# A decoder layer on one core: interleaving hi and lo of the stationary operands and reading the moving ones backwards in both FFNs

## The chip, the cores and the metric

The kernel runs on one core of a Trainium2 chip. TensorE multiplies: a matmul holds one operand still in its array (the stationary one, read from SBUF by a weight load of 128 columns, shown in the trace as PEld LDWEIGHTS) and streams the other (the moving one) past it, one column after the other; the sums go to PSUM. VectorE (DVE), ScalarE (ACT) and GpSimd (POOL) work element by element, SyncE (SP) starts most transfers. SBUF has 128 partitions; what is said below of places and steps is within a partition, in elements of four bytes.

The metric is the device time of one execution in microseconds. A profile is one execution with records of every instruction.

## The reference

One layer with 16 meta tokens and 256 sequence tokens, 272 positions of 2048 features, all in float32:

```python
h = h + 0.5 * swiglu(rms_norm(h, ffn1_norm_g), ffn1_w_gate, ffn1_w_up, ffn1_w_down)
u = rms_norm(h, mix_norm_g); z = u @ w_in          # q, k, v, q_idx, k_idx, w_idx, x_c, B, C, two gates
# sparse attention: the 64 best keys per query by an indexer, softmax over them
# short gated convolution; both branches gated, summed, projected
h = h + merged @ w_out
h = h + 0.5 * swiglu(rms_norm(h, ffn2_norm_g), ffn2_w_gate, ffn2_w_up, ffn2_w_down)
return h[:, N_META:]
```

with `swiglu(x, g, u, d) = (silu(x @ g) * (x @ u)) @ d` and 5632 hidden features. Each weight matrix is used once.

## The kernel before

Every matmul operand of the large products is split into a high part (the value rounded to the type float32r, which TensorE streams at full rate) and a low part (what is left). A product is then three matmuls, hi*hi, hi*lo and lo*hi, added up in the same PSUM bank.

*The stream of weights.* The class `Stream` (L68 on) carries all weights in the order of use. `load` brings chunks of 128 x 2048 elements from HBM into three raw buffers (L100, issued by SP). `split` (L106) takes blocks of 1024 columns: ACT writes the high part into a tile `whi` (L115), DVE the low part into a tile `wlo` (L116), four buffers of each. `next` hands out blocks in order, splits three blocks ahead (`AHEAD`), and runs the small work of other engines that was queued with `later` for that block. So TensorE's order is the program's order, and ACT and DVE work ahead of it by blocks.

*FFN 1* (`ffn_features`, L430) keeps features on partitions. The weights are stationary, 128 x 128 at a time, the activations are moving, 272 tokens at a time: `fmajor` (L292) calls `mac` (L286), whose three matmuls are L288 (whi with the high activations), L289 (whi with the low ones) and L290 (wlo with the high ones). The activations lie in `act` (L226), for each of 16 feature tiles a high and a low row of `PITCH` = 320 elements; the 272 tokens fill places 48 to 319, so that they end on a multiple of `LINE` = 64. The hidden features go to `mid` (L435) in rows of the same kind, in two halves (c = 0, 1) of 22 tiles; gate, up and down products are `pg`, `pu`, `pd`. The first two gate and up tiles run interleaved as `start_tiles`. `norm` (L391) adds the squares over partitions with two small matmuls against ones (L403); their result scales the columns of the gate and up products.

*The middle* (projections, attention, convolution, branches, output projection) uses the same stream, `fmajor`, `paired` and `tokens`. Its last step, `to_act` (L1056), writes the normed input of FFN 2, high and low part, back into the rows of `act`.

*FFN 2* (`ffn_tokens`, L487) has the roles exchanged: activations are stationary, 128 features x 128 tokens, and the weights move, 512 columns at a time. `tokens` (L308) issues for each of the two token tiles j and each block the three matmuls L316 (xhi, whi), L317 (xhi, wlo), L318 (xlo, whi). The stationary operands come from `act` through `act_tokens` (L321) for gate and up, and from `mid` (L490) for down; `mid` holds per feature tile 256 high elements and then 256 low ones, written by `split_into` (L339) at L535.

In both FFNs, high and low parts of a stationary operand lie in separate runs, each read with step one, and a stationary tile begins at a multiple of 64 elements of its SBUF tile. Every moving operand is read in ascending order.

Of the kernel before, what the change touches and what calls it, by code (L numbers as in the profile page):

```python
# [10 lines left out]
F32R = mybir.dt.float32r  # L11
# [51 lines left out]
LATER = LINE - META  # L63
SUB = 1024
RAW = 2048


class Stream:  # L68
# [14 lines left out]

    def add(self, src, n, width, cuts=()):

        per = min(SUB // width, SUB // P)
        g = len(self.loads)
        self.loads.append((src, n * width, cuts))
        at = [0, *cuts, n] if cuts else [*range(0, n, per), n]
        for a, b in zip(at, at[1:]):  # L90
            self.subs.append((g, a * width, b - a, width))

# [13 lines left out]
    def split(self, upto):  # L106
        nc = self.nc
        while self.n_split < min(upto, len(self.subs)):
            g, c, kk, width = self.subs[self.n_split]
            self.load(g + RAW_BUFS)  # L110
            n = kk * width
            raw = self.raw[g][:, c : c + n]
            hi = self.split_pool.tile([P, SUB], F32R, name="whi")
            lo = self.split_pool.tile([P, SUB], F32R, name="wlo")
            nc.scalar.activation(hi[:, :n], raw, AF.Copy)  # L115
            nc.vector.tensor_sub(lo[:, :n], raw, hi[:, :n].bitcast(F32))  # L116
            self.ready[self.n_split] = [
                (hi[:, i * width : (i + 1) * width], lo[:, i * width : (i + 1) * width]) for i in range(kk)
            ]
            self.n_split += 1  # L120
            if self.n_split == len(self.subs) or self.subs[self.n_split][0] > g:
                self.load(g + 1 + RAW_BUFS)
# [39 lines left out]
def tile_decoder_layer(  # L162
# [31 lines left out]

    def chunks(src, i0, i1, width=P):
        for i in range(i0, i1):
            st.add(src[i], RAW // width, width)

    st.add(wgu1[0], RAW // P, P, (4, 8, 12))
    st.add(wgu1[1], RAW // P, P, (4, 8))  # L200
    for c in range(2):
        chunks(wgu1, max(2, c * 2 * FHALF), (c + 1) * 2 * FHALF)
        chunks(wd1, c * FHALF, (c + 1) * FHALF)
    chunks(wk, 0, G)
# [102 lines left out]

    def tokens(ps_of, x, n):  # L308

        k = 0  # L310
        while k < n:
            blocks = [st.next()] + st.rest()
            for j, ps in ps_of.items():
                for i, (whi, wlo) in enumerate(blocks):
                    xhi, xlo = x(k + i, j, 0), x(k + i, j, 1)
                    nc.tensor.matmul(ps, xhi, whi, start=k + i == 0, stop=False)  # L316
                    nc.tensor.matmul(ps, xhi, wlo, start=False, stop=False)  # L317
                    nc.tensor.matmul(ps, xlo, whi, start=False, stop=k + i == n - 1)  # L318
            k += len(blocks)
# [70 lines left out]

    def norm(row, lag, cols=False):  # L391

        box = {}

        def two(x):
            return x.rearrange("p (a t) -> p a t", a=2)

        def total():
            nc.vector.tensor_add(ssq[0], ssq[0], ssq[1])

        def across():
            for i in range(2):
                nc.tensor.matmul(row[:, i], ones, two(ssq[0])[:, i], start=True, stop=True)  # L403
            box[0] = rsqrt(two(R), row, (P, T), 1.0 / D, two)

        def inverse():
            box[0][1]()
            if cols:
                nc.vector.tensor_mul(R2, R, R)
                turned(rcol[:, 0], R[:, :32], 0, 0)  # L410
                for q in range(4):
                    turned(
                        rcol[:, 1:3], R[:, META:].rearrange("p (j r b) -> p r j b", r=4, b=32)[:, q], q, q
                    )

        st.later(total, lag)
        st.early(across, lag + 1)
        st.later(lambda: box[0][0](), lag + 1)
        st.later(inverse, lag + 2)
# [10 lines left out]
    def ffn_features():  # L430

        n = T
        xhi, xlo = parts(LATER)
        with tc.tile_pool(name="ffn1", bufs=2, reuse_waits="tile") as fp:
            mid = fp.tile([P, FHALF, 2, PITCH], F32R, name="mid", bufs=1)  # L435
            i_hi, i_lo = (mid[:, :, i, PITCH - n :] for i in range(2))

# [13 lines left out]
            two = [aux_tile(f"start{i}") for i in range(2)]  # L451
            norm(two[0][:, :, T : T + T // 2], 13)
            least = st.at + 14
            for c in range(2):
                for f in range(FHALF):
# [13 lines left out]
                    st.later(lambda pu=pu, box=box: times(pu, box), 1 + side, least + 1)  # L469
                    st.later(lambda f=f, box=box: split_into(i_hi[:, f, :], i_lo[:, f, :], box["v"]), 2 + side, least + 1)  # L470
                for d in range(KD):
                    pd = mm_tile("pd")
                    fmajor(pd[:, :n], lambda k: i_hi[:, k, :], lambda k: i_lo[:, k, :], FHALF)
                    st.later(lambda d=d, pd=pd: add_to(h[:, d], pd, 0.5, False))
                    if c == 1:
                        st.later(lambda d=d: (next_act(d, gains[1], 0, LATER), square(d, 0)), 2)

    def turn_columns(mt, s, r):
# [8 lines left out]
    def ffn_tokens():  # L487

        with tc.tile_pool(name="ffn2", bufs=1, reuse_waits="tile") as fp:
            mid = fp.tile([P, 4 * GROUPS[0], 2, SEQ], F32R, name="mid")  # L490

# [30 lines left out]
            for c, n in enumerate(GROUPS):  # L522
                for f in range(n):
                    s = fp.tile([P, 2, 512], F32, name="s", bufs=2)
                    mt = fp.tile([P, 4, SEQ], F32, name="mt", bufs=2)
                    pg = {j: mm_tile(f"pg{j}") for j in (1, 2)}
                    tokens(pg, act_tokens, KD)
                    st.later(lambda pg=pg, s=s: gate(pg, s))
                    pu = {j: mm_tile(f"pu{j}") for j in (1, 2)}
                    tokens(pu, act_tokens, KD)  # L530
                    st.later(lambda pu=pu, s=s: times(pu, s))
                    for r in range(4):
                        st.later(lambda mt=mt, s=s, r=r: turn_columns(mt, s, r), 2 + r)
                    to = mid[:, 4 * f : 4 * f + 4]
                    st.later(lambda to=to, mt=mt: split_into(to[:, :, 0], to[:, :, 1], mt), 6)  # L535
                for d in range(D // 512):
                    pd = {j: mm_tile(f"pd{j}") for j in (1, 2)}
                    tokens(pd, lambda k, j, part: mid[:, k, part, (j - 1) * P : j * P], 4 * n)
                    for j in (1, 2):
# [24 lines left out]
    with ExitStack() as mix:  # L564
# [491 lines left out]
        def to_act(g, mt):  # L1056
            for f in range(4):
                d = 4 * g + f
                hi, lo = (act[:, d, i, LATER + META :][:, :SEQ] for i in range(2))
                gain = gains[2][:, d : d + 1]  # L1060
# [48 lines left out]


def _down_columns(w):
    cut = GROUPS[0] * 512
    return np.concatenate([_chunks(_tiles(w[:cut], 512)), _chunks(_tiles(w[cut:], 512))])

# [30 lines left out]
def _layout(x, meta_tokens, ffn1_norm_g, ffn1_w_gate, ffn1_w_up, ffn1_w_down, mix_norm_g, w_in, q_norm_g,  # L1145
# [31 lines left out]
    a["wo"] = _chunks(_tiles(w_out[0], 512))  # L1177
    gu = np.stack([_tiles(ffn2_w_gate[0], 512), _tiles(ffn2_w_up[0], 512)], 1)
    a["wgu2"] = _chunks(gu.reshape(-1, P, KD * 512))
# [21 lines left out]
```

## Time and profile before

| | |
|---|---|
| median of two runs | 2143.46 us (2143.18 to 2143.74) |
| span of the profiled execution | 2141.4 us |
| DMA | 397.58 MB, mean 186 GB/s |
| matmuls and weight loads recorded | 12902 each |
| FFN 1 | about 5 to 788 us of the span |
| middle | 788 to 1419 us |
| FFN 2 | 1419 us to the end |

The page of the profile begins with the busy time of each engine and its share of the span. Busy time of TensorE is no measure of its speed, because a matmul's record lasts longer than the distance to the next one: consecutive matmuls overlap. What matters on a TensorE that never waits is that distance, called a slot here. The page's groups (line, engine, operation, result<-operands, shapes, count | busy time, mean time of one in ns | idle time of the engine before them and what ended it) show counts and means; the view of stretches gives busy time and counts between two moments.

### The profile page before, as it was taken

To read this page: it belongs to the slowest core of one execution; us is meant where nothing else is said; L and a number is where in the kernel's file an instruction comes from. 1 tells how busy PE (TensorE), PEld (TensorE's weight loads), DVE (VectorE), ACT (ScalarE), POOL (GpSimd) and SP (SyncE) were. 2 spreads that over 40 slices of the span, in tenths; PEclk is the share of its full clock that TensorE was granted. 3 is DMA by queue.
4 is the path that set the end of the run, shared out by engine and by line. 5 is a ranking of instruction groups with operands and counts; after the bars stand their busy time and mean duration, and the time that the engine had idled before them with its cause. 6 is when DMAs were issued, how large, how long until landed. Compare 5 with 4: busy or idle time off the path is not lost.

```text
span 2141.4 us, 30929 instructions
## 1 busy us (share of the span) xinstructions
PE 2136.3 (100%) x12902; PEld 1921.2 (90%) x12902; DVE 1325.8 (62%) x1776; ACT 954.5 (45%) x1173; POOL 10.0 (0%) x28
## 2 busy tenths in 40 slices
PE   9999999999999999999999999999999999999999
PEld 9999999999999998799988888888888888888887
DVE  7555544455555556677686487886676644666664
ACT  6444433344444445565444444454444433444442
POOL 0000000000000000000000000000000000000000
PEclk9999999999999999999999999999999999999999
DMA  7555545555544545454555555555555555555554
GB/s 267 189 181 179 179 180 178 178 177 177 177 178 178 177 170 177 159 176 158 172 188 194 194 189 204 177 183 210 196 196 186 196 191 195 196 197 195 189 200 143
DMA packets 56909, 397.58 MB, mean 186 GB/s; under 512 B 6337, under 2 KB 7105, under 8 KB 9409
## 3 DMA queue, kind: packets, MB, share of 16 engines
q1 hardware_dynamic: 55872, 393.51, 53.4%
q8 instruction: 101, 1.65, 0.3%
q10 hardware_dynamic: 576, 1.05, 0.1%
q0 software_dynamic: 320, 1.05, 0.1%
q14 instruction: 40, 0.32, 0.0%
HBM read 393.49 MB, written 2.10 MB: 185 GB/s over the span
## 4 chain that ended last, share of the span: by engine, by line
PE 99%; DMA 0%; DVE 0%; SPq 0%; ACT 0%; issue 0%; ACTq 0%
PE pd L290 4%; PE pd L289 4%; PE pd L288 4%; PE pu L289 4%; PE pg L289 4%; PE pg L288 4%; PE pu L288 4%; PE pu L290 4%; PE pg L290 4%; PE pg L317 4%; PE pg L318 4%; PE pd L318 4%; PE pu L317 4%; PE pg L316 4%; PE pu L316 4%; PE pd L316 4%
## 5 line engine op out<-in xcount | busy, mean ns | idle before, releaser
L116 DVE TENSOR_TENSOR wlo<-raw,whi 128x1024 fp32r<-128x1024 f32 (+1 forms) x749 | 912.7, 1220 | 780.6 <-ACT whi L115 777.6
L115 ACT ACTIVATE whi<-raw 128x1024 fp32r<-128x1024 f32 (+1 forms) x749 | 788.3, 1055 | 1079.2 <-PE pd L289 146.3
L288 PE MATMUL pd<-mid,whi 128*128 128x272 f32 x704 | 201.7, 286 | 0.0
L289 PE MATMUL pd<-mid,whi 128*128 128x272 f32 x704 | 201.7, 286 | 0.0
L290 PE MATMUL pd<-mid,wlo 128*128 128x272 f32 x704 | 201.7, 286 | 0.0
L288 PE MATMUL pu<-act,whi 128*128 128x272 f32 x672 | 192.6, 287 | 0.0
L289 PE MATMUL pu<-act,whi 128*128 128x272 f32 x672 | 192.5, 287 | 0.0
L288 PE MATMUL pg<-act,whi 128*128 128x272 f32 x672 | 192.5, 286 | 0.0
L289 PE MATMUL pg<-act,whi 128*128 128x272 f32 x672 | 192.5, 286 | 0.0
L290 PE MATMUL pg<-act,wlo 128*128 128x272 f32 x672 | 192.5, 286 | 0.0
L290 PE MATMUL pu<-act,wlo 128*128 128x272 f32 x672 | 192.5, 286 | 0.0
L317 PE MATMUL pg<-wlo,act 128*128 128x512 f32 x352 | 137.2, 390 | 0.0
L318 PE MATMUL pg<-whi,act 128*128 128x512 f32 x352 | 137.1, 389 | 0.0
L316 PE MATMUL pg<-whi,act 128*128 128x512 f32 x352 | 136.9, 389 | 0.0
L316 PE MATMUL pu<-whi,act 128*128 128x512 f32 x352 | 136.9, 389 | 0.0
L317 PE MATMUL pu<-wlo,act 128*128 128x512 f32 x352 | 136.9, 389 | 0.0
L318 PE MATMUL pu<-whi,act 128*128 128x512 f32 x352 | 136.9, 389 | 0.0
L316 PE MATMUL pd<-whi,mid 128*128 128x512 f32 x352 | 136.9, 389 | 0.0
L317 PE MATMUL pd<-wlo,mid 128*128 128x512 f32 x352 | 136.9, 389 | 0.0
L318 PE MATMUL pd<-whi,mid 128*128 128x512 f32 x352 | 136.9, 389 | 0.0
L288 PEld LDWEIGHTS pd<-mid,whi 128*128 128x128 f32 x704 | 132.6, 188 | 0.0
L289 PEld LDWEIGHTS pd<-mid,whi 128*128 128x128 f32 x704 | 132.6, 188 | 0.0
(248 smaller groups left out, 4014.3 us busy)
## 6 DMA issues: line engine op xcount, KB each, us to landing
raw<-in_wgu_dram SPq DMA_DIRECT2D x174, 1024.0 KB, 4.8
raw<-in_wd_dram SPq DMA_DIRECT2D x88, 1024.0 KB, 4.8
raw<-in_wcv_dram SPq DMA_DIRECT2D x24, 1024.0 KB, 4.8
raw<-in_wgc_dram SPq DMA_DIRECT2D x24, 1024.0 KB, 4.9
raw<-in_wga_dram SPq DMA_DIRECT2D x24, 1024.0 KB, 4.8
raw<-in_wo_dram SPq DMA_DIRECT2D x16, 1024.0 KB, 4.8
raw<-in_wqi_dram SPq DMA_DIRECT2D x8, 1024.0 KB, 4.9
raw<-in_wq_dram SPq DMA_DIRECT2D x8, 1024.0 KB, 4.8
```

Source lines behind the costliest of these rows:

```text
L115: nc.scalar.activation(hi[:, :n], raw, AF.Copy)
L116: nc.vector.tensor_sub(lo[:, :n], raw, hi[:, :n].bitcast(F32))
L288: nc.tensor.matmul(ps, whi, xhi, start=first, stop=False)
L289: nc.tensor.matmul(ps, whi, xlo, start=False, stop=False)
L290: nc.tensor.matmul(ps, wlo, xhi, start=False, stop=last)
L316: nc.tensor.matmul(ps, xhi, whi, start=k + i == 0, stop=False)
L317: nc.tensor.matmul(ps, xhi, wlo, start=False, stop=False)
L318: nc.tensor.matmul(ps, xlo, whi, start=False, stop=k + i == n - 1)
```

## The change

Nothing is computed differently, and the count of instructions and transfers is meant to stay.

- In FFN 1 the high and low part of a weight block lie in one tile, element by element in turn (hi, lo, hi, lo), from a start `mesh` that goes with the number of the chunk: `i % 64` for gate and up (0 for the first four), `3 * i % 64` for down. All other weights keep high and low part in two runs, now in one tile of 2 x 1024 + 64 elements.
- In FFN 2 the activations are laid out likewise: in `act`, with a start from `STILL` by pairs of feature tiles, and in `mid`, with a start from `MIDDLE` by groups of four.
- The moving operands of both FFNs are read from the last element to the first. In FFN 1 these are the activations, so the gate and up products have their tokens in reverse; the norm's row is made in reverse too, `mid` is stored in reverse, and the down product, which reads `mid` backwards, has the tokens in order again. In FFN 2 these are the weights; the host stores each run of 512 columns in reverse.
- The second half of FFN 1's `mid` lies 16 elements lower.

```diff
+STILL = 0, 1, 2, 4, 8, 16, 32, 64
+MIDDLE = 0, 3, 12, 24, 40, 48
...
-            hi = self.split_pool.tile([P, SUB], F32R, name="whi")
-            lo = self.split_pool.tile([P, SUB], F32R, name="wlo")
+            both = self.split_pool.tile([P, 2 * SUB + LINE], F32R, name="w")
+            if mesh is None:
+                hi, lo = both[:, :SUB], both[:, SUB : 2 * SUB]
+            else:
+                hi, lo = (both[:, mesh : mesh + 2 * SUB].rearrange("p (c i) -> p i c", i=2)[:, i] for i in range(2))
...
-    def chunks(src, i0, i1, width=P):
+    def chunks(src, i0, i1, width=P, mesh=lambda i: None):
         for i in range(i0, i1):
-            st.add(src[i], RAW // width, width)
-
-    st.add(wgu1[0], RAW // P, P, (4, 8, 12))
-    st.add(wgu1[1], RAW // P, P, (4, 8))
+            st.add(src[i], RAW // width, width, mesh=mesh(i))
+
+    st.add(wgu1[0], RAW // P, P, (4, 8, 12), 0)
+    st.add(wgu1[1], RAW // P, P, (4, 8), 0)
     for c in range(2):
-        chunks(wgu1, max(2, c * 2 * FHALF), (c + 1) * 2 * FHALF)
-        chunks(wd1, c * FHALF, (c + 1) * FHALF)
+        chunks(wgu1, max(2, c * 2 * FHALF), (c + 1) * 2 * FHALF, mesh=lambda i: i % LINE if i > 3 else 0)
+        chunks(wd1, c * FHALF, (c + 1) * FHALF, mesh=lambda i: 3 * i % LINE)
...
-    def tokens(ps_of, x, n):
+    def tokens(ps_of, x, n, back=False):
...
             blocks = [st.next()] + st.rest()
+            if back:
+                blocks = [(whi[:, ::-1], wlo[:, ::-1]) for whi, wlo in blocks]
...
-                nc.tensor.matmul(row[:, i], ones, two(ssq[0])[:, i], start=True, stop=True)
+                x = two(ssq[0])[:, 1 - i, ::-1] if back else two(ssq[0])[:, i]
+                nc.tensor.matmul(row[:, i], ones, x, start=True, stop=True)
...
-        xhi, xlo = parts(LATER)
+        xhi, xlo = (lambda k, f=f: f(k)[:, ::-1] for f in parts(LATER))
...
-            i_hi, i_lo = (mid[:, :, i, PITCH - n :] for i in range(2))
+            ends = [PITCH, PITCH - 16]
+            i_hi, i_lo = ([mid[:, :, i, e - n : e] for e in ends] for i in range(2))
...
-                    fmajor(pd[:, :n], lambda k: i_hi[:, k, :], lambda k: i_lo[:, k, :], FHALF)
+                    fmajor(pd[:, :n], lambda k: i_hi[c][:, k, ::-1], lambda k: i_lo[c][:, k, ::-1], FHALF)
...
+    def last_part(k, i):
+        at = STILL[k // 2]
+        x = act[:, k].rearrange("p i t -> p (i t)")[:, at : at + 2 * SEQ]
+        return x.rearrange("p (t i) -> p i t", i=2)[:, i]
+
+    def last_tokens(k, j, part):
+        return last_part(k, part)[:, (j - 1) * P : j * P]
...
-            mid = fp.tile([P, 4 * GROUPS[0], 2, SEQ], F32R, name="mid")
+            mid = fp.tile([P, 4 * GROUPS[0], 2 * SEQ + LINE], F32R, name="mid")
+
+            def middle(f):
+                at = MIDDLE[f]
+                x = mid[:, 4 * f : 4 * f + 4, at : at + 2 * SEQ]
+                return x.rearrange("p k (t i) -> p k i t", i=2)
...
-                    tokens(pg, act_tokens, KD)
+                    tokens(pg, last_tokens, KD, True)
...
-                    tokens(pd, lambda k, j, part: mid[:, k, part, (j - 1) * P : j * P], 4 * n)
+                    tokens(pd, lambda k, j, part: middle(k // 4)[:, k % 4, part, (j - 1) * P : j * P], 4 * n, True)
...
-                hi, lo = (act[:, d, i, LATER + META :][:, :SEQ] for i in range(2))
+                hi, lo = (last_part(d, i) for i in range(2))
...
+def _back(tiles):
+
+    return tiles.reshape(*tiles.shape[:2], -1, 512)[..., ::-1].reshape(tiles.shape)
```

More of the change, by code (lines that the diff above doesn't have):

```diff
@@ L82, in __init__, with add @@
         self.first = []
-    def add(self, src, n, width, cuts=()):
+    def add(self, src, n, width, cuts=(), mesh=None):
         per = min(SUB // width, SUB // P)
@@ L90, in add @@
         for a, b in zip(at, at[1:]):
-            self.subs.append((g, a * width, b - a, width))
+            self.subs.append((g, a * width, b - a, width, mesh))
     def load(self, upto, between=(), queues=()):
@@ L108, in split @@
         while self.n_split < min(upto, len(self.subs)):
-            g, c, kk, width = self.subs[self.n_split]
+            g, c, kk, width, mesh = self.subs[self.n_split]
             self.load(g + RAW_BUFS)
@@ L389, in turned, with norm @@
         nc.vector.transpose(dst[rows * 32 : rows * 32 + 32], src[cols * 32 : cols * 32 + 32])
-    def norm(row, lag, cols=False):
+    def norm(row, lag, cols=False, back=False):
         box = {}
@@ L451, in ffn_features @@
             two = [aux_tile(f"start{i}") for i in range(2)]
-            norm(two[0][:, :, T : T + T // 2], 13)
+            norm(two[0][:, :, T : T + T // 2], 13, back=True)
             least = st.at + 14
@@ L469, in ffn_features @@
                     st.later(lambda pu=pu, box=box: times(pu, box), 1 + side, least + 1)
-                    st.later(lambda f=f, box=box: split_into(i_hi[:, f, :], i_lo[:, f, :], box["v"]), 2 + side, least + 1)
+                    st.later(lambda f=f, c=c, box=box: split_into(i_hi[c][:, f, :], i_lo[c][:, f, :], box["v"]), 2 + side, least + 1)
                 for d in range(KD):
                     pd = mm_tile("pd")
-                    fmajor(pd[:, :n], lambda k: i_hi[:, k, :], lambda k: i_lo[:, k, :], FHALF)
+                    fmajor(pd[:, :n], lambda k: i_hi[c][:, k, ::-1], lambda k: i_lo[c][:, k, ::-1], FHALF)
                     st.later(lambda d=d, pd=pd: add_to(h[:, d], pd, 0.5, False))
@@ L526, in ffn_tokens @@
                     pg = {j: mm_tile(f"pg{j}") for j in (1, 2)}
-                    tokens(pg, act_tokens, KD)
+                    tokens(pg, last_tokens, KD, True)
                     st.later(lambda pg=pg, s=s: gate(pg, s))
                     pu = {j: mm_tile(f"pu{j}") for j in (1, 2)}
-                    tokens(pu, act_tokens, KD)
+                    tokens(pu, last_tokens, KD, True)
                     st.later(lambda pu=pu, s=s: times(pu, s))
@@ L533, in ffn_tokens @@
                         st.later(lambda mt=mt, s=s, r=r: turn_columns(mt, s, r), 2 + r)
-                    to = mid[:, 4 * f : 4 * f + 4]
+                    to = middle(f)
                     st.later(lambda to=to, mt=mt: split_into(to[:, :, 0], to[:, :, 1], mt), 6)
@@ L1108, in _down @@
     return _chunks(np.concatenate([_tiles(w[: FF // 2], P), _tiles(w[FF // 2 :], P)]))
+def _back(tiles):
+    return tiles.reshape(*tiles.shape[:2], -1, 512)[..., ::-1].reshape(tiles.shape)
 def _down_columns(w):
     cut = GROUPS[0] * 512
-    return np.concatenate([_chunks(_tiles(w[:cut], 512)), _chunks(_tiles(w[cut:], 512))])
+    return np.concatenate([_chunks(_back(_tiles(x, 512))) for x in (w[:cut], w[cut:])])
 def _branch(gate, w):
@@ L1177, in _layout @@
     a["wo"] = _chunks(_tiles(w_out[0], 512))
-    gu = np.stack([_tiles(ffn2_w_gate[0], 512), _tiles(ffn2_w_up[0], 512)], 1)
+    gu = np.stack([_back(_tiles(w, 512)) for w in (ffn2_w_gate[0], ffn2_w_up[0])], 1)
     a["wgu2"] = _chunks(gu.reshape(-1, P, KD * 512))
```

## The prediction

> **What bounds the kernel now.** I read the page first: the busy time, the clock and the chain that ended last.
>
> ```profile
> span 2141.4 us, 30929 instructions
> PE 2136.3 (100%) x12902; PEld 1921.2 (90%) x12902; DVE 1325.8 (62%) x1776; ACT 954.5 (45%) x1173; POOL 10.0 (0%) x28
> PEclk9999999999999999999999999999999999999999
> PE 99%; DMA 0%; DVE 0%; SPq 0%; ACT 0%; issue 0%; ACTq 0%
> ```
>
> TensorE is never idle, its clock is granted in full, and the chain lies on it for 99% of the span. So the time is a sum of slots: the distance from the start of one matmul to the start of the next. The change adds no instruction and takes none away; what it can alter is the length of a slot. Busy time does not show slots, since matmuls overlap; they come from the busy times of two long stretches, the first inside FFN 1 and the second inside FFN 2.
>
> ```profile
> core 0: us, PE busy (x) PEld busy (x) DVE busy (x) ACT busy (x) POOL busy (x), PEclk, DMA share, GB/s
> 30.00:788.40 758.40, 758.40 (x6150) 758.23 (x6149) 408.22 (x504) 315.31 (x381) 0.32 (x1) 1.00 0.52 179
> 1440.00:2040.00 600.00, 600.00 (x2649) 496.82 (x2648) 375.73 (x436) 258.71 (x256) 0.00 (x0) 1.00 0.57 195
> ```
>
> A stretch counts about two matmuls that only reach into it, so FFN 1 has 758.4 / 6148 = 123.4 ns for a slot of 272 columns, and FFN 2 has 600 / 2647 = 226.7 ns for one of 512. Per column that is (226.7 - 123.4) / 240 = 0.43 ns, and 6.3 ns for each matmul besides. How many slots there are follows from the groups:
>
> ```profile
> L288 PE MATMUL pd<-mid,whi 128*128 128x272 f32 x704 | 201.7, 286 | 0.0
> L288 PE MATMUL pu<-act,whi 128*128 128x272 f32 x672 | 192.6, 287 | 0.0
> L288 PE MATMUL start<-act,whi 128*128 128x272 f32 x64 | 18.4, 288 | 0.2 <-ACT whi L115 0.2
> L316 PE MATMUL pg<-whi,act 128*128 128x512 f32 x352 | 136.9, 389 | 0.0
> ```
>
> Each stands for three products (hi*hi, hi*lo, lo*hi), and pg has as many as pu in FFN 1 and the three of pg, pu, pd are alike in FFN 2: 3 x (704 + 2 x 672 + 64) = 6336 slots in FFN 1 and 9 x 352 = 3168 in FFN 2, 782 and 718 us, 70% of the span. One nanosecond on every FFN slot is 9.5 us. The 2% that a measurement of this kernel can tell from no change is 43 us, or 4.5 ns on each of these slots.
>
> **What hides beside the matmuls.** A slot holds a weight load for the next matmul. These rows give its price by column.
>
> ```profile
> L288 PEld LDWEIGHTS pd<-mid,whi 128*128 128x128 f32 x704 | 132.6, 188 | 0.0
> L288 PEld LDWEIGHTS pkv<-act,whi 128*80 128x80 f32 x16 | 2.4, 148 | 0.0
> ```
>
> 48 columns fewer are 40 ns less, 0.83 ns a column, so 128 columns are read in 107 ns, and the rest of the 188 is latency. In FFN 1 that leaves 16 ns of the slot free, in FFN 2 120 ns. Is there more in a slot than its own columns? An f32 matmul in the attention tells:
>
> ```profile
> 997.45 0.86 PE ppv L888 x2
> L888 PE MATMUL ppv<-pTx,vts 128*128 128x512 f32 x4 | 2.1, 613 | 0.0
> ```
>
> Two of 512 columns took 0.86 us, 0.84 ns a column. At half of that, if the rounded type of the FFNs streams twice as fast with nothing else in the way, 512 columns would be 215 ns and 272 would be 114. The slots are 11.7 and 9.2 ns longer. That excess is where place, step and direction can act, in either direction.
>
> **The change part by part.** *ACT and DVE write with a step of two elements.* The splits of FFN 1's weights (L115, L116), FFN 2's mid (L340, L341) and the writes of act at L1061 keep their counts and lengths.
>
> ```profile
> L115 ACT ACTIVATE whi<-raw 128x1024 fp32r<-128x1024 f32 x741 | 783.0, 1059 | 1073.6 <-PE pd L289 146.3 <-PE pu L289 139.3 <-PE pg L289 137.2
> L116 DVE TENSOR_TENSOR wlo<-raw,whi 128x1024 fp32r<-128x1024 f32 x741 | 906.9, 1226 | 777.7 <-ACT whi L115 774.8
> 101.84 1.06 ACT L115 ACTIVATE whi<-raw 128x1024 fp32r<-128x1024 f32 x1 [1.59 <-PE pu L289]
> 104.79 1.06 ACT L115 ACTIVATE whi<-raw 128x1024 fp32r<-128x1024 f32 x1 [1.89 <-PE pg L289]
> ```
>
> A block of 1024 columns feeds 24 slots, 2.95 us, and ACT stands still for more than half of it until TensorE frees a buffer. No row has such a step. Below: nothing, since these engines already take about 1 ns an element. Above: twice as long, 2.1 and 2.5 us a block, under 2.95 still, with three blocks split ahead as cover. I take nothing. Without that cover it would be (2.45 - 1.23) x about 265 blocks, 320 us; only a DVE beyond twice its present time would uncover it.
>
> *One tile holds hi and lo.* The first matmul on a block may now wait for the DVE's lo too, and the buffer is free only when both parts are read (one slot later at most). Three blocks ahead, that is hidden; at the start it is not:
>
> ```profile
> 12.94 1.07 ACT whi L115
> 14.04 1.24 DVE wlo L116
> 15.31 0.39 PE start L290
> ```
>
> PE waits there for lo one or two matmuls after it began on hi; it would now wait with the first. Nothing to 1.5 us in all (the lo is due in any case); I take 0.5.
>
> *Queues and loads.* No transfer is added, moved or resized: the reversed order of FFN 2's weight columns and the order back for the output are made in the host's layout. The weight loads were the same 188 ns throughout, under a DMA share of 0.5, so I count nothing. The norm's two reversed matmuls of 136 columns (L403) occur once.
>
> *Stationary operands: step two, and off their 64-element grid.* Before, each stationary tile of the FFNs began at a multiple of 64 elements of its tile. The one group that leaves that grid is the 80-column k_idx group, with starts at multiples of 80; its 48 slots run from the first of these rows to the last:
>
> ```profile
> 800.97 0.29 PE L288 MATMUL pkv<-act,whi 128*80 128x272 f32 x1
> ...
> 806.98 0.29 PE L288 MATMUL pkv<-act,whi 128*128 128x272 f32 x1
> ```
>
> 6.01 / 48 = 125.2 ns against 123.4: 1.8 ns more, although it loads fewer columns. The moving operand has such a row as well, the convolution's 258 columns from element 62 on:
>
> ```profile
> 971.73 0.28 PE L288 MATMUL pxc<-act,whi 128*128 128x258 f32 x1
> ...
> 972.69 0.28 PE L290 MATMUL pxc<-act,wlo 128*128 128x258 f32 x1
> ```
>
> 0.96 / 8 = 120 ns, where 258 x 0.43 + 6.3 is 117.3: 2.7 ns more. So a slot does depend on where its operands lie, by some 2 ns, and up in both rows. For FFN 1 I take the first, the nearest (same columns, same lines): 6336 x 1.8 = 11.4 us. For FFN 2 the load has 120 ns free instead of 16; I take nothing, with 0 to 3168 x 1.8 = 5.7 us as bounds. The step of two has no row: it could remove all of the excess (-95 us, below) or double it (+95 us); between ends that far apart I stay with the rows just named, which lie near zero.
>
> The Trainium skill, page "SBUF — State Buffer", section "Door 1: The DMA port swizzle", says that SBUF is read in lines of 16 bytes and that two accesses to one line suffice for full bandwidth. A step of two fp32 elements meets that exactly, so by the page the interleaving is free and the sum is the time before, 2143.5. No run here shows a step of two yet.
>
> *Moving operands backwards.* Same elements, same ends in FFN 1's act (the slice still lies on the same lines), 16 elements off in the second half's mid; FFN 2's weights stay on the grid. No row reads backwards. Between nothing and the half rate of the f32 row (price below) I take nothing, because the pieces fetched are the same.
>
> **Sum.** 11.4 + 0 + 0.5 = 12 us on a profiled execution of 2141.4 us; the median of the runs is 2143.5, 2 us above that span. So 2143.5 + 12 = 2155.5, taken as 2156.
>
> **The rivals.**
> *Nothing moves.* Every pattern is read at the same rate, and the 1.8 ns of the k_idx group belong to its 80 columns. For it: in FFN 1 the slots average 123.4 over 6148, whatever ACT, DVE and the DMAs were doing. Against it: the two rows above. 2143.5.
>
> *The excess goes.* The 9.2 and 11.7 ns are two streams getting in each other's way while both climb through SBUF; when one runs down and the other goes at twice its former pace in bytes, they cross quickly. For it: the f32 row has no such excess. Against: a part of it may be a fixed cost per matmul. All of it gone is 6336 x 9.2 + 3168 x 11.7 = 58 + 37 = 95 us: 2048. Half is 2096, faster by 2.2%.
>
> The page "TensorE: Matmul & The Clock Gate", section "Part 2: What happens when you issue a matmul", gives the load and the moving operand a read port each that do not disturb one another, so by it there would be nothing to gain here. It is a rule for "nothing moves"; the excess in the rows speaks against its reading that nothing disturbs.
>
> *The excess doubles.* An interleaved 128-column load covers 1024 bytes where it covered 512, so it fetches twice as many pieces, and each is one more chance to hold up the moving stream. The other side of the forecast: +95 us, 2238, slower by 4.4%; half of it, 2191, already decides for slower (from 4.5 ns a slot).
>
> *A rate halves.* Either the interleaved load takes twice as long (213 ns: FFN 1's slot becomes that, 6336 x 90 = +570 us, 2714, FFN 2 still covers it), or the backward stream goes at the f32 rate (229 and 430 ns: 6336 x 106 + 3168 x 203 = +1315 us). The load decides from 16 ns more on. Nothing in the trace speaks for it but that no row excludes it.
>
> **How the numbers follow.** Forecast (a nanosecond or two a slot) 0.28, with its own range of 2143 to 2172; nothing moves 0.20; the excess goes, at least by half, 0.22; it doubles, at least by half, 0.20; a rate halves 0.10. So faster 0.22, same 0.48, slower 0.30. A range from 2075 to 2240 leaves out the halved rates and the lowest third of the gain, 0.17.
>
> **What would show it.** The same two stretches of the changed kernel: slots near 125 and 227 ns for the forecast, 118 and below with 220 for the gain, 128 and more for the loss. A load of FFN 1 with a mean clearly above 188 ns would be the halved load. Slots that differ between stretches with different offsets show that place matters; equal ones that the step or the direction does. Means of L115 and L116 above twice 1059 and 1226 ns, or idle time before FFN matmuls, would break the cover that I count on. The forecast is wrong if the slots outside the FFNs move, since nothing there is changed.

## The result and the profile after

| | before | after |
|---|---|---|
| median | 2143.46 us | 2174.3 us (2174.06 to 2174.54) |
| ratio after / before | | 1.0144, 95% interval 1.0115 to 1.0174 |
| span of the profiled execution | 2141.4 us | 2172.8 us |

The changed kernel is 31 us slower, well outside its measurement and inside the 2% that the prediction called no change. The first lines of its page, with its clock row and the chain that ended last:

```profile
span 2172.8 us, 30770 instructions
PE 2167.3 (100%) x12902; PEld 1955.9 (90%) x12902; DVE 1326.8 (61%) x1776; ACT 985.4 (45%) x1173; POOL 10.0 (0%) x28
PEclk9999999999999999999999999999999999999999
PE 99%; DMA 1%; DVE 0%; SPq 0%; ACT 0%; issue 0%; ACTq 0%
```

TensorE has the same 12902 matmuls, the clock is still full, and the chain is still TensorE for 99%. (The 159 instructions fewer are semaphore instructions of DVE.) So nearly all of the 31 us must be longer slots. The two stretches of the prediction show where; the columns are those of its own fence (busy time and count of PE, PEld, DVE, ACT and POOL, then clock, DMA share, GB/s).

```profile
30.00:788.40 758.40, 758.40 (x6073) 758.25 (x6072) 402.92 (x497) 340.26 (x377) 0.32 (x1) 1.00 0.51 178
1440.00:2040.00 600.00, 600.00 (x2573) 502.36 (x2572) 368.81 (x436) 254.08 (x253) 0.00 (x0) 1.00 0.56 189
```

With two matmuls off each count again, FFN 1 has 758.4 / 6071 = 124.9 ns a slot (123.4 before) and FFN 2 has 600 / 2571 = 233.4 ns (226.7 before). In the list of all matmul starts of the two traces the means over the whole FFNs are 123.37 and 124.91, 226.83 and 233.34. Times the counts: 3168 x 6.51 = 20.6 us in FFN 2 and 6144 x 1.54 = 9.5 us in FFN 1 (its 192 start slots apart). All other matmuls together went from 660.1 to 661.3 us. That is the 31 us: two thirds of it in FFN 2, where the prediction had put nothing, and 1.2 us outside these slots.

The groups that answer to the prediction's, from the page of the changed kernel:

```profile
L295 PE MATMUL pd<-mid,w 128*128 128x272 f32 x704 | 203.3, 289 | 0.0
L323 PE MATMUL pu<-w,act 128*128 128x512 f32 x352 | 139.9, 397 | 0.0
L295 PEld LDWEIGHTS pd<-mid,w 128*128 128x128 f32 x704 | 137.3, 195 | 0.0
```

A matmul's record is 3 to 8 ns longer (286 and 389 before) and a load's 7 ns (188 before); the idle column is 0.0, as before. Nothing waits.

ACT and DVE, as grouped in the stretch from 100 to 780 us of FFN 1. First ACT in the kernel before:

```profile
L115 ACT ACTIVATE whi<-raw 128x1024 fp32r<-128x1024 f32 x230 | 243.7, 1059 | 403.2 <-PE pd L289 141.3 <-PE pu L289 124.5 <-PE pg L289 124.1
```

Then ACT and DVE in the changed kernel, two answers of the same view:

```profile
L120 ACT ACTIVATE w<-raw 128x1024 fp32r<-128x1024 f32 x227 | 267.9, 1180 | 382.1 <-PE pd L295 130.4 <-PE pu L295 123.3 <-PE pg L295 120.7
L121 DVE TENSOR_TENSOR w<-raw,w 128x1024 fp32r<-128x1024 f32 x228 | 280.0, 1228 | 328.4 <-ACT w L120 328.4
```

Writing every second element costs ACT 121 ns a block and DVE nothing (1226 before). ACT still stands idle for 382 of these 680 us, nearly all of it until TensorE frees a buffer, and DVE for 328 until ACT's part is there, so it stays hidden.

The start of FFN 1, where the lo part is waited for. The rows of TensorE in the kernel before, in order of time:

```profile
14.93 0.28 PE L289 MATMUL start<-act,whi 128*128 128x272 f32 x1
15.31 0.39 PE L290 MATMUL start<-act,wlo 128*128 128x272 f32 x1
```

And in the changed kernel:

```profile
15.40 0.29 PE L294 MATMUL start<-act,w 128*128 128x272 f32 x1
15.99 0.41 PE L295 MATMUL start<-act,w 128*128 128x272 f32 x1 [0.31 <-DVE w L121]
```

The gap over a plain slot was 0.38 - 0.12 = 0.26 us and is 0.59 - 0.12 = 0.47 us: 0.2 us more. The wait still stands before the third product, not before the first as the prediction had it, and the same wait at the first block became 0.16 us shorter.

### The profile page after: what moved, and what is told of

It is laid out like the page before. It is cut to its first block, busy times and chain, and to the rows that moved or that the text cites. A ratio compares the mean times of both kernels' runs of the same rounds, so it can differ in the third digit from the quotient of the medians.

```text
span 2172.8 us, 30770 instructions
## 1 busy us (share of the span) xinstructions
PE 2167.3 (100%) x12902; PEld 1955.9 (90%) x12902; DVE 1326.8 (61%) x1776; ACT 985.4 (45%) x1173; POOL 10.0 (0%) x28
## 4 chain that ended last, share of the span: by engine, by line
PE 99%; DMA 1%; DVE 0%; SPq 0%; ACT 0%; issue 0%; ACTq 0%
PE pd L294 4%; PE pd L295 4%; PE pd L293 4%; PE pu L293 4%; PE pg L293 4%; PE pg L295 4%; PE pu L294 4%; PE pu L295 4%; PE pg L294 4%; PE pd L325 4%; PE pg L325 4%; PE pd L323 4%; PE pg L324 4%; PE pu L325 4%; PE pu L324 4%; PE pu L323 4%
## 5 line engine op out<-in xcount | busy, mean ns | idle before, releaser
L121 DVE TENSOR_TENSOR w<-raw,w 128x1024 fp32r<-128x1024 f32 (+1 forms) x749 | 913.1, 1220 | 809.9 <-ACT w L120 806.8
L120 ACT ACTIVATE w<-raw 128x1024 fp32r<-128x1024 f32 (+1 forms) x749 | 820.2, 1097 | 1083.9 <-PE pd L295 140.2
L295 PE MATMUL pd<-mid,w 128*128 128x272 f32 x704 | 203.3, 289 | 0.0
L294 PE MATMUL pd<-mid,w 128*128 128x272 f32 x704 | 203.1, 289 | 0.0
L293 PE MATMUL pd<-mid,w 128*128 128x272 f32 x704 | 202.9, 288 | 0.0
L293 PE MATMUL pu<-act,w 128*128 128x272 f32 x672 | 193.9, 289 | 0.0
L294 PE MATMUL pu<-act,w 128*128 128x272 f32 x672 | 193.9, 289 | 0.0
L294 PE MATMUL pg<-act,w 128*128 128x272 f32 x672 | 193.9, 289 | 0.0
L293 PE MATMUL pg<-act,w 128*128 128x272 f32 x672 | 193.9, 289 | 0.0
L295 PE MATMUL pg<-act,w 128*128 128x272 f32 x672 | 193.8, 288 | 0.0
L295 PE MATMUL pu<-act,w 128*128 128x272 f32 x672 | 193.7, 288 | 0.0
L323 PE MATMUL pu<-w,act 128*128 128x512 f32 x352 | 139.9, 397 | 0.0
L324 PE MATMUL pu<-w,act 128*128 128x512 f32 x352 | 139.9, 397 | 0.0
L325 PE MATMUL pu<-w,act 128*128 128x512 f32 x352 | 139.9, 397 | 0.0
L323 PE MATMUL pd<-w,mid 128*128 128x512 f32 x352 | 139.9, 397 | 0.0
L324 PE MATMUL pd<-w,mid 128*128 128x512 f32 x352 | 139.9, 397 | 0.0
L325 PE MATMUL pd<-w,mid 128*128 128x512 f32 x352 | 139.9, 397 | 0.0
L324 PE MATMUL pg<-w,act 128*128 128x512 f32 x352 | 139.9, 397 | 0.0
L323 PE MATMUL pg<-w,act 128*128 128x512 f32 x352 | 139.9, 397 | 0.0
L325 PE MATMUL pg<-w,act 128*128 128x512 f32 x352 | 139.9, 397 | 0.0
L295 PEld LDWEIGHTS pd<-mid,w 128*128 128x128 f32 x704 | 137.3, 195 | 0.0
L293 PEld LDWEIGHTS pd<-mid,w 128*128 128x128 f32 x704 | 137.2, 195 | 0.0
```

Of the source, the lines that this page charges most:

```text
L293: nc.tensor.matmul(ps, whi, xhi, start=first, stop=False)
L294: nc.tensor.matmul(ps, whi, xlo, start=False, stop=False)
L295: nc.tensor.matmul(ps, wlo, xhi, start=False, stop=last)
```

## The experiments

The change has three edits: stationary operands are **interleaved** (or lie apart), the moving ones run **backwards** (or forwards), and the **places** vary (or lie on the 64-element grid). Places below are in elements of four bytes, modulo 64. The first four runs undo one edit each or leave one; all are cut from the changed kernel unless it says otherwise. "Slots" are the means over an FFN of the distances between matmul starts, FFN 1 / FFN 2; the rows of the stretches give the same within 0.1 ns. In e1_forward, e2_apart, e4_places and e6_back_places the second half of FFN 1's mid stays 16 elements lower, as in the changed kernel.

| run | stationary | moving | places of the stationary | median us | ratio [95%] | slots, ns |
|---|---|---|---|---|---|---|
| before | apart | forwards | grid | 2143.3 | | 123.37 / 226.83 |
| after | interleaved | backwards | varied | 2174.3 | 1.0144 [1.0115, 1.0174] | 124.91 / 233.34 |
| e1_forward | interleaved | forwards | varied | 2179.3 | 1.0169 [1.0153, 1.0184] | 126.25 / 232.37 |
| e2_apart | apart | backwards | grid | 2174.7 | 1.0148 [1.0132, 1.0163] | 125.07 / 233.34 |
| e3_grid | interleaved | backwards | grid | 2185.2 | 1.0196 [1.0181, 1.0211] | 126.69 / 233.33 |
| e4_places | apart | forwards | varied | 2169.9 | 1.0124 [1.0107, 1.0141] | 125.41 / 231.18 |
| e5_step | interleaved | forwards | grid | 2191.6 | 1.0218 [1.0203, 1.0234] | 126.68 / 233.33 |
| e6_back_places | apart | backwards | varied | 2176.3 | 1.0153 [1.0136, 1.0170] | 125.38 / 233.33 |

**One edit undone, or one alone.** e1_forward takes the reading backwards away, in both FFNs, the norm and the host's layout:

```diff
-        xhi, xlo = (lambda k, f=f: f(k)[:, ::-1] for f in parts(LATER))
+        xhi, xlo = parts(LATER)
...
-                    tokens(pg, last_tokens, KD, True)
+                    tokens(pg, last_tokens, KD)
...
-    return tiles.reshape(*tiles.shape[:2], -1, 512)[..., ::-1].reshape(tiles.shape)
+    return tiles
```

> The changed kernel with both FFNs' moving operands read forwards again; the interleaving and the varied places stay. In the changed kernel the slots are 124.9 ns in FFN 1 and 233.3 in FFN 2, +31 us in all, 21 of them in FFN 2. Theory step (the interleaved load holds up the moving stream): slots stay near 125 and 233.3, time about 2174 us. Rival direction (reading backwards costs): 123.4 and 226.7, about 2143 us. Rival place: slots vary with the start of the stationary tile, and the time stays above 2143 by what the changed places cost.

e2_apart keeps the reading backwards, and the lower second half of mid; hi and lo lie apart, every other place is 0:

```diff
-STILL = 0, 1, 2, 4, 8, 16, 32, 64
-MIDDLE = 0, 3, 12, 24, 40, 48
+STILL = 0, 0, 0, 0, 0, 0, 0, 0
+MIDDLE = 0, 0, 0, 0, 0, 0
...
-                hi, lo = (both[:, mesh : mesh + 2 * SUB].rearrange("p (c i) -> p i c", i=2)[:, i] for i in range(2))
+                hi, lo = (both[:, mesh + i * SUB : mesh + (i + 1) * SUB] for i in range(2))
...
-        return x.rearrange("p (t i) -> p i t", i=2)[:, i]
+        return act[:, k, i, at : at + SEQ]
```

> The changed kernel with high and low parts in separate runs on the 64-element grid; the moving operands stay backwards, and the second half of FFN 1's mid stays 16 elements lower. Theory step: 123.4 and 226.7 ns, about 2143 us. Rival direction: about 125 and 233.3, about 2174 us.

e3_grid puts every stationary operand's place, and the second half's mid, back on the grid, still interleaved and backwards:

```diff
-STILL = 0, 1, 2, 4, 8, 16, 32, 64
-MIDDLE = 0, 3, 12, 24, 40, 48
+STILL = 0, 0, 0, 0, 0, 0, 0, 0
+MIDDLE = 0, 0, 0, 0, 0, 0
...
-            ends = [PITCH, PITCH - 16]
+            ends = [PITCH, PITCH]
```

> The changed kernel with every place set to 0: interleaved, backwards, on the grid. Step or direction: FFN 2 stays at 233.3 ns at every tile (it did not differ between starts in the changed kernel), time 2165 to 2174 us. Rival place: both slots fall to 123.4 and 226.7, 2143 us.

e4_places has the edits of e1_forward and those of e2_apart that lay hi and lo apart: only the places vary.

> Separate runs and forwards as before, but the stationary tiles at the varied places and the second half of FFN 1's mid 16 lower. The prediction's step (a start off the grid costs 1.8 ns in FFN 1, nothing in FFN 2): 125.2 and 226.7 ns, about 2155 us. Theory step or direction alone: 123.4 and 226.7, 2143 us. Place alone: about 2174 us.

The stretches of e1_forward, e2_apart, e3_grid and e4_places, two rows each, in this order:

```profile
30.00:788.40 758.40, 758.40 (x6009) 758.34 (x6008) 398.79 (x491) 327.72 (x371) 0.32 (x1) 1.00 0.50 176
1440.00:2040.00 600.00, 600.00 (x2584) 502.07 (x2584) 371.88 (x445) 255.39 (x257) 0.00 (x0) 1.00 0.56 190
```

```profile
30.00:788.40 758.40, 758.40 (x6067) 758.40 (x6066) 401.36 (x495) 310.20 (x374) 0.32 (x1) 1.00 0.51 177
1440.00:2040.00 600.00, 600.00 (x2573) 483.44 (x2572) 368.16 (x436) 253.27 (x253) 0.00 (x0) 1.00 0.55 188
```

```profile
30.00:788.40 758.40, 758.40 (x5988) 758.30 (x5988) 397.86 (x490) 341.47 (x370) 0.32 (x1) 1.00 0.50 175
1440.00:2040.00 600.00, 600.00 (x2573) 506.58 (x2572) 371.05 (x444) 254.98 (x256) 0.00 (x0) 1.00 0.56 189
```

```profile
30.00:788.40 758.40, 758.40 (x6050) 758.40 (x6050) 401.27 (x494) 310.13 (x373) 0.32 (x1) 1.00 0.51 177
1440.00:2040.00 600.00, 600.00 (x2597) 487.89 (x2596) 371.20 (x441) 255.72 (x256) 0.00 (x0) 1.00 0.56 189
```

Read the counts: the fewer matmuls begin in 600 us, the longer the slot. e2_apart has the count of the changed kernel in FFN 2 to the last one (2573) and nearly in FFN 1 (6067 against 6073), with the backward reading: that edit by itself is worth the whole 31 us. (Of FFN 1's down slots, those of the lowered second half took 125.3 ns and those of the first 125.0, which is 0.4 us in all.) Yet the count doesn't go back to 2649 without it: e1_forward (2584) is no faster. And places alone (e4_places, 2597) cost 27 us. The varied places are not always a loss: e3_grid, which takes them out of the changed kernel, is 11 us slower than it, all in FFN 1 (126.69 against 124.91 ns). The edits don't add up.

**The other corners.** Is the step harmless when nothing else changes, and do places matter backwards? e5_step joins the edits of e1_forward and e3_grid; e6_back_places has only the `hi, lo` line and `act[:, k, i, at : at + SEQ]` of e2_apart.

> Interleaved, but forwards and with every place on the grid: the step alone. Rival additive (each of the three edits has a price of its own, and the changed kernel would be their sum): since direction alone gave 125.1 and 233.3 ns and places alone 125.4 and 231.2, the step must cost about nothing, 123.4 and 226.7, 2143 us. Theory settled order (before, the two streams stand in one favourable position to each other; whatever moves either of them out of it costs nearly the whole price): 125 to 127 ns and 231 to 234, 2165 to 2185 us.

> Separate runs, read backwards, at the varied places. Rival additive: direction and places add up, FFN 1 127, FFN 2 238 ns, about 2200 us. Theory settled order: once the moving stream runs backwards the place no longer matters in FFN 2, 233.3 ns at every start, FFN 1 124.5 to 126, 2172 to 2180 us.

The stretches of e5_step, then of e6_back_places:

```profile
30.00:788.40 758.40, 758.40 (x5989) 758.35 (x5989) 397.59 (x490) 324.45 (x369) 0.32 (x1) 1.00 0.50 175
1440.00:2040.00 600.00, 600.00 (x2573) 496.31 (x2572) 370.78 (x444) 254.16 (x256) 0.00 (x0) 1.00 0.56 189
```

```profile
30.00:788.40 758.40, 758.40 (x6051) 758.18 (x6050) 401.68 (x495) 310.29 (x374) 0.32 (x1) 1.00 0.51 177
1440.00:2040.00 600.00, 600.00 (x2573) 483.44 (x2572) 368.71 (x439) 253.42 (x254) 0.00 (x0) 1.00 0.56 188
```

Interleaving alone is the worst of all, +48 us by the median. (Three of its four times lie near 2192 and the profiled one at 2185.0; the slots are those of the latter.) Backwards, FFN 2 is at 2573 whatever the step and the places of the stationary operand: its slot then has a length of its own, 233.33 ns, and the prices of the other two edits vanish in it. Within the changed kernel too, the mean of FFN 2's slots is 233.3 ns at every place. Forwards, they follow the place. Means of FFN 2's slots in e4_places, by the place where the stationary operand starts (mean of pg, pu and pd where several have it):

```
start     0      1      2      3      4      8      12     16     24     32     40     48
ns      227.6  231.8  230.8  226.9  233.0  233.1  233.2  233.1  234.1  233.2  233.8  229.4
```

The load's own record doesn't show this; in e4_places it is as long as before:

```profile
L323 PEld LDWEIGHTS pg<-w,act 128*128 128x128 f32 x340 | 63.9, 188 | 14.5
```

**What of a load is it: its length or where it lies?** If the price lay in the length of a load, it should fall with the load's columns. e7_few is the kernel before with the second and third product of each step loading only 80 columns, the first of the 128; e8_few_back is e2_apart with the same, and with the second half of mid back in its place.

```diff
+        m = whi.shape[1] if first or last else min(few, whi.shape[1])
...
-        nc.tensor.matmul(ps, whi, xlo, start=False, stop=False)
-        nc.tensor.matmul(ps, wlo, xhi, start=False, stop=last)
+        nc.tensor.matmul(ps[:m], whi[:, :m], xlo, start=False, stop=False)
+        nc.tensor.matmul(ps[:m], wlo[:, :m], xhi, start=False, stop=last)
```

> The kernel before with loads of 80 instead of 128 columns for the second and third product of each step in both FFNs (first and last step of a sum left whole); what is left out are those two products for 48 of 128 output rows. If the excess over 114 and 215 ns is the load getting in the way of the moving stream, it shrinks with the columns: slots in which 80 columns are loaded fall from 123.4 to about 120 and from 226.7 to about 222, in all 2143 - 2/3 x (6336 x 3.4 + 3168 x 4.4) = about 2120 us. If the excess is a fixed cost of a matmul or of its columns, nothing falls: 2143 us.

> The same shorter loads, in separate runs on the grid, with the moving operands backwards (alone with whole loads: 125.1 and 233.3 ns). If direction acts through the load, slots in which 80 columns are loaded lose more than in the forward case (18.4 ns of excess in FFN 2, 80/128 of it is 11.5: about 226; FFN 1 about 121), about 2138 us. If reading backwards has a cost of its own, they stay 6.7 ns above the forward kernel with the same loads in FFN 2.

e7_few became slower, 2174.2 us (1.0144 [1.0129, 1.0159]), with 125.45 / 232.58 ns; e8_few_back took 2177.6 us (1.0160 [1.0145, 1.0176]), with 125.49 / 233.34. Loading less cost 31 us forwards, and backwards FFN 2 kept its count of 2573. So it isn't the length. In FFN 1 of e7_few the slots in which 80 columns are loaded last 126.6 ns and those in which 128 are loaded 123.8. In FFN 2 the two kinds differ less, 233.0 and 232.0 ns: there the slots with a whole load became longer too, by 5 ns, though their own load had not changed. Length is not all that differs, though: 80 columns that start on the grid end off it. e9_few_end loads the last 80 of the 128 instead, so that the load starts off the grid and ends where it did before:

```diff
-        nc.tensor.matmul(ps[:m], whi[:, :m], xlo, start=False, stop=False)
+        at = whi.shape[1] - m
+        nc.tensor.matmul(ps[:m], whi[:, at:], xlo, start=False, stop=False)
```

> As the run with loads of 80 columns, but the last 80 of each 128 (columns 48 to 127) instead of the first 80, so that the load ends on the 64-element grid and begins off it; the two products of these columns are added to output rows 0 to 79. That run had 126.6 ns in FFN 1 where 80 columns were loaded and 231.4 to 234.6 in FFN 2. Theory end (what counts is where the last column of the load lies to the grid): 123.4 and 226.7 ns, about 2143 us. Rival width (80 columns cost by themselves): 126.6 and 233, about 2174 us. Rival start (what counts is where the first column lies): places like those of the run with varied places, 125 to 126 and 229 to 234, 2165 to 2180 us.

It took 2149.8 us (1.0030 [1.0018, 1.0042]). The stretches of e7_few, then of e8_few_back and of e9_few_end:

```profile
30.00:788.40 758.40, 758.40 (x6048) 758.31 (x6047) 401.16 (x495) 309.46 (x372) 0.32 (x1) 1.00 0.51 177
1440.00:2040.00 600.00, 600.00 (x2581) 423.64 (x2580) 369.61 (x440) 254.21 (x254) 0.00 (x0) 1.00 0.56 189
```

```profile
30.00:788.40 758.40, 758.40 (x6046) 758.40 (x6045) 400.62 (x494) 309.07 (x373) 0.32 (x1) 1.00 0.51 176
1440.00:2040.00 600.00, 600.00 (x2573) 422.80 (x2572) 369.41 (x442) 252.19 (x253) 0.00 (x0) 1.00 0.55 188
```

```profile
30.00:788.40 758.40, 758.40 (x6097) 758.40 (x6096) 404.65 (x499) 312.86 (x377) 0.32 (x1) 1.00 0.52 178
1440.00:2040.00 600.00, 600.00 (x2647) 434.36 (x2646) 374.64 (x439) 261.68 (x261) 0.00 (x0) 1.00 0.57 194
```

The same number of columns, loaded from 48 elements further up, gives FFN 2 its 226.8 ns back (2647 against 2581) and FFN 1 about half of its loss (124.5 ns). So in FFN 2 it isn't the length, and a start off the grid does no harm there by itself. What e9_few_end shares with the kernel before, and e7_few doesn't, is the end of the load. As a rule for every place that doesn't stand: in e4_places loads that start at 3, and end at 2, are as fast (226.9 ns). And in FFN 1 one of the two short loads costs as much in e9_few_end as in e7_few: the slots between the first and the second product last 126.5 and 126.6 ns.

**The moving operand's place.** e10_moving leaves everything as before but the places of the moving operands: FFN 2's weight blocks start at 0 to 63 by their chunk, FFN 1's mid at 32 and 16 instead of 48. e11_moving_back does the same backwards (mid ends 8 and 32 lower).

```diff
-        chunks(wgu2, gu, gu + 8 * n, 512)
-        chunks(wd2, down, down + 4 * n, 512)
+        chunks(wgu2, gu, gu + 8 * n, 512, lambda i: i % LINE)
+        chunks(wd2, down, down + 4 * n, 512, lambda i: 3 * i % LINE)
...
-            ends = [PITCH, PITCH - 16]
+            ends = [PITCH - 16, PITCH - 32]
```

> Separate runs, forwards, stationary tiles on the grid; FFN 2's weights, which move, lie at 0 to 63 elements off the grid by chunk, and the moving operand of FFN 1's down products at 32 and at 16 instead of 48. Theory relative (only the distance between the two streams counts): slots like those with varied stationary places, 227 to 235 in FFN 2 with a mean near 231, about 2160 us. Rival own grid (the moving stream's own place counts): a pattern that the stationary places did not show. A slot below 226.7 ns or 123.3 ns at some place would point to a kernel faster than before.

> The same moved places, read backwards; the moving operand of FFN 1's down products lies at 40 and at 16. Theory backwards has its own rate (233.3 ns in FFN 2 whatever the step, the place and the length of the load): 233.3 at all 64 places, about 2175 us. Rival: the constant came from the one place that all backward runs shared, and moving it makes the slots vary, with values down to 226.7.

e10_moving took 2170.6 us (1.0126 [1.0109, 1.0143]), e11_moving_back 2180.5 (1.0173 [1.0158, 1.0188]). The stretches of e10_moving, then of e11_moving_back:

```profile
30.00:788.40 758.40, 758.40 (x6096) 758.38 (x6095) 404.22 (x499) 312.14 (x378) 0.32 (x1) 1.00 0.52 178
1440.00:2040.00 600.00, 600.00 (x2577) 485.73 (x2576) 367.53 (x434) 254.23 (x254) 0.00 (x0) 1.00 0.55 189
```

```profile
30.00:788.40 758.40, 758.40 (x6079) 758.40 (x6078) 403.25 (x497) 311.40 (x376) 0.32 (x1) 1.00 0.52 178
1440.00:2040.00 600.00, 600.00 (x2547) 481.72 (x2547) 364.36 (x432) 250.48 (x250) 0.00 (x0) 1.00 0.55 187
```

Forwards, only the blocks at place 0 keep 226.9 ns; the others have 227.8 (at 7 and 15) to 239.7. Those that start three past a multiple of four elements have 227.8 to 231.9, those one past it 233.5 to 239.7. In FFN 1 pg and pu, whose act wasn't moved, stay at 123.4 and pd, whose mid was, goes to 126.67 at both new places. Since this kernel keeps its weights in the changed kernel's wider tile, the same figures show that the tile by itself costs next to nothing. Backwards, 233.33 ns turns out to be a floor and not the only value: the blocks that start at 16 or 28, whose first element read lies at 15 or 27, have it to the hundredth, others go up to 241.5, and none has a mean below. Thirteen of the sixteen starts at a multiple of four lie within 0.25 ns of the floor, all other starts at 233.7 ns or more.

**Step two with its end where it was.** The last run asks whether the interleaving costs by itself or only because it moves the end of the load: e12_step_end is e5_step with every place 1, so that the hi loads (two of three) end on element 63 of the grid, as before.

```diff
-STILL = 0, 1, 2, 4, 8, 16, 32, 64
-MIDDLE = 0, 3, 12, 24, 40, 48
+STILL = 1, 1, 1, 1, 1, 1, 1, 1
+MIDDLE = 1, 1, 1, 1, 1, 1
```

> Interleaved and forwards as in the run with the step alone, but with every place at 1 instead of 0: the last column of a high tile then lies on element 63 of the 64-element grid (at 62 before), that of a low tile on 0. With every place at 0 the slots were 126.7 and 233.3 ns, 2185 to 2192 us. Theory end alone (the step itself is free, the place of the load's last column decides): two loads of three now end where they ended in the kernel before, so FFN 2 falls to 227 to 230 ns and FFN 1 to 123.5 to 125.5, about 2145 to 2165 us. Rival step (the interleaved load costs by itself): 233 and 126 to 127 as with place 0, 2180 us or more.

It took 2178.0 us (1.0162 [1.0144, 1.0180]), with slots of 126.69 / 231.15. Its stretches:

```profile
30.00:788.40 758.40, 758.40 (x5988) 758.33 (x5988) 397.62 (x490) 325.34 (x370) 0.32 (x1) 1.00 0.51 175
1440.00:2040.00 600.00, 600.00 (x2597) 503.44 (x2596) 374.44 (x447) 256.65 (x258) 0.00 (x0) 1.00 0.55 190
```

FFN 1 is where e5_step had it, and FFN 2 got back 2.2 of its 6.5 ns. With step two FFN 2's mean slot doesn't come near 226.7 at any of the places tried: it is 231.2 ns here, and 230.3 at the best place in e1_forward, 16. So, forwards, the step costs beside the place.

## Why the prediction was right, and where it was wrong

The time is in the range and on the side that was forecast, 18 us above the number. The slots are the cause, as it said, but much of the rest is luck. The forecast by itself reached from 2143 to 2172 us, and 2174.3 lies 2 us above that: the full range, 2075 to 2240, held the time because it made room for rivals as well. And the sum of 12 us has FFN 1 nearly right and FFN 2, where 20.6 us came, at nothing.

- **What bounds the kernel: right.** Every difference between the kernels here is a count of matmuls in a stretch. The matmuls outside the FFNs moved by 1.2 us in 660.
- **"Moving operands backwards ... I take nothing, because the pieces fetched are the same": the step that failed.** e2_apart measured 6.5 ns x 3168 = 20.6 us in FFN 2 and 1.7 ns x 6144 = 10.4 us in FFN 1 for the direction (0.4 us of it from the lowered second half of mid). The same elements from the same lines don't take the same time. Its bounds (nothing, half the rate) held this; the choice of the lower one, with no row for it, did not.
- **"For FFN 2 the load has 120 ns free instead of 16; I take nothing": failed too.** Free time behind the load was to protect the slot. It doesn't: forwards, places alone took 226.8 to 231.2 (e4_places), 4.4 x 3168 = 13.8 us, and the step alone to 233.3 (e5_step), with the load's own record unchanged at 188 ns in the first of them. The upper bound of 5.7 us, carried over from FFN 1, was far too low.
- **FFN 1's 11.4 us: the size was right, the sum by luck.** 1.8 ns a slot were predicted for the places, 1.54 came for all three edits; places alone cost 2.0 (e4_places). But the step alone cost 3.3 (e5_step) and the direction 1.7 (e2_apart), both taken at nothing, and only together do the three come to 1.54. And the row it was priced from, the k_idx group, mixes two things that were not told apart: its loads have 80 columns, and they begin and end elsewhere. e7_few and e9_few_end show that with 80 columns a shift of the place takes away about half of the price in FFN 1, so reading the row as a price of place was fair in part; that it would apply to FFN 1 alone was not.
- **A sum of edits: wrong in form.** Direction alone is worth 31 us, places alone 27, the step alone 42 in the profiled execution, and all three together 31. In FFN 2 that is because a backward stream has its floor at 233.33 ns, above most of what place and step do forwards; why FFN 1 doesn't add up either, I can't say.
- **ACT, DVE, queues, start: right in effect.** 121 ns a block for ACT where nothing was taken, nothing for DVE, both hidden. At the start one wait for lo grew by 0.2 us and another shrank by 0.16, for the 0.5 taken.
- **The rivals.** "Nothing moves" and "the excess goes" fell: averaged over the three products at one place, no kernel had a slot below the 123.3 and 226.7 ns of before. "A rate halves" fell: the loads went from 188 to 195 ns only, and the slots stayed far from 229 and 430 ns. "The excess doubles" had the right sign in FFN 2, 11.7 to 18.3 ns. Its mechanism, an interleaved load that holds up the moving stream, is not needed there, since e2_apart has the same 233.34 ns without interleaving; but e5_step shows that forwards the step alone costs as much. That it does so by fetching more pieces is shown by no run.

The Trainium skill's page "SBUF — State Buffer", section "Door 1: The DMA port swizzle", made the interleaving free by its rule of two accesses to a 16-byte line. The runs disagree: 126.68 and 233.33 ns in e5_step, against 123.37 and 226.83. The Trainium skill's page "TensorE: Matmul & The Clock Gate", section "Part 2: What happens when you issue a matmul", gives load and moving stream a port each; by that, where a load lies could not matter to a slot that it doesn't fill. e9_few_end and e7_few disagree, with 226.8 and 232.6 ns for the same 80 columns.

What stays open: whether the two reads get into each other's way, and by what resource of SBUF or TensorE; for the backward floor it may be the moving stream alone. No trace shows a single read. Nor is it known why FFN 2's slots with an unchanged load became longer in e7_few. That the end of a load counts in FFN 2 would fit a load that is read from its last column to its first, but no run shows the direction of a load, and it doesn't explain the good place 3.

## What to carry to other kernels

Keep the operands of a TensorE that never waits plain: step one, ascending, with loads that begin and end on the 64-element grid and moving operands that end on it, as in the kernel before. Here every other kernel cost between 0.3% and 2.2% of the time, though single places off the grid (3) were as good. Measure such an edit in each stage and alone, because the prices don't add, and because free time behind the load protected nothing here. And look at the distance between matmul starts: the share of busy time (100% before and after) and the idle columns (0.0) show nothing of the 31 us.

## What the runs showed of the hardware that was not expected

- A moving operand of 512 columns read backwards never took less than 233.33 ns a slot in the mean of any place, against 226.67 forwards at the best; that holds for stationary operands interleaved or apart, at every place tried, and with 80 or 128 columns loaded.
- The slots that stay the same from one to the next are multiples of 3.33 ns: 123.33, 126.67 (pd in e5_step), 226.67 and 233.33 are 37, 38, 68 and 70 of it. At other places the slots change from one to the next (225 to 250 ns in FFN 2 of e10_moving).
- Loading fewer columns can make a kernel slower: e7_few by 31 us, of which e9_few_end, with as many columns loaded from another place, has 6.5.
- ACT's write with a step of two costs 121 ns on 1059 for 1024 elements beside backward matmuls, where the same write with step one costs nothing beside the same matmuls. ACT in e2_apart:

```profile
L120 ACT ACTIVATE w<-raw 128x1024 fp32r<-128x1024 f32 x227 | 240.3, 1059 | 408.6 <-PE pd L295 139.6 <-PE pu L295 131.6 <-PE pg L295 128.9
```

- With step two it depends on the direction in which TensorE reads: 1138 ns in e5_step, forwards, and 1207 in e3_grid, backwards. These are ACT's rows in e5_step and in e3_grid:

```profile
L120 ACT ACTIVATE w<-raw 128x1024 fp32r<-128x1024 f32 x224 | 254.9, 1138 | 395.7 <-PE pd L295 132.9 <-PE pu L295 129.3 <-PE pg L295 126.6
```

```profile
L120 ACT ACTIVATE w<-raw 128x1024 fp32r<-128x1024 f32 x224 | 270.4, 1207 | 380.6 <-PE pd L295 127.9 <-PE pu L295 124.5 <-PE pg L295 121.6
```
